# A gated product on one core: the first tile's first row is stored in two halves

## The chip, the cores and the metric

The kernel runs on one core of a Trainium2 chip. The metric is the device time of one execution in microseconds (us), the median of the runs shown. The core has engines that work side by side (VectorE, here DVE; ScalarE, ACT; GpSimd, POOL; SyncE, SP; TensorE is not used) and 16 DMA engines that move data between the chip's memory and the core's on-chip buffer. A transfer is issued by an engine's instruction stream, here SP's for loads and ACT's for stores, and signals on a semaphore when it has landed.

## The reference

```python
def reference(x):                       # x: 8192 x 8192, float32
    a, b = np.split(x, 2, axis=-1)
    return a * (1 / (1 + np.exp(-b)))   # 8192 x 4096, float32
```

Each row of `x` has 8192 numbers. The first half is multiplied by the sigmoid of the second half. 268.4 MB are read and 134.2 MB written.

## The kernel before, in words

**Tiles.** The 8192 rows are cut into 32 tiles of 256 rows (L20). A tile lies on the 128 partitions of the on-chip buffer, two rows of `x` to a partition (`R = 2`), so a tile's load is 8 MB (64 KB to a partition) and its store 4 MB (32 KB to a partition). There are two input slots `x_sb0`, `x_sb1` and two output slots `o_sb0`, `o_sb1`; tile i uses slot i mod 2 (`SLOTS = 2`).

**Pieces.** A tile's work, loads and stores are cut in units of which a tile has eight: 0 to 4 is the first row of every partition, 4 to 8 the second. For tiles 1 to 30 the load is one transfer, the work is two pieces (3/16 of the columns and the other 13/16, over both rows), and the store is one transfer. Tile 0 is loaded in two transfers of a row each, worked in four pieces of half a row each (`fourths`) and stored in two transfers of a row each. The last tile is worked in fourths too and stored in three transfers: a row, half a row, half a row.

**One piece** (`work`, L72): ACT replaces the second half of the row by its sigmoid, in place (L82), then DVE multiplies both halves into the output slot (L84). From tile 2 on POOL does the product of the smaller piece in place of DVE.

**What waits for what.** The order of instructions on each engine is the order in which the program writes them (`place` keeps program order), and `place` declares which waits are kept:

- A load of tile i + 2 (L63, issued by SP) waits for the products of tile i that read the same slot. The first three transfers, tile 0's two and tile 1's one, wait for nothing.
- A sigmoid waits for the load of its piece. For tiles 1 to 30 it also waits for the store of tile i - 2 that last read this output slot, if there is one; so tile 2's sigmoid waits for all of tile 0's stores, tile 3's for tile 1's store, and so on.
- A product waits for its sigmoid.
- A store (L68, issued by ACT's stream) waits for the products that it stores. ACT's stream is in order: while a store's issue waits for a product, the sigmoids behind it wait too.

**The order of the stores.** After piece k of a tile the loop at L98 issues those stores that are ready, but never after the last piece; the rest are issued after the next load. `behind[i]` (L36) says how many pieces a store's issue is held back: with 0 a store is issued as soon as the last piece that it needs has been written to the program, with 1 it is issued one piece later, so that the sigmoid of the following piece stands ahead of it in ACT's stream. For tile 0 (`behind` 0) the order on ACT is: sigmoid 0, sigmoid 1, store of row 0, sigmoid 2, sigmoid 3, store of row 1. For the last tile `behind` is 1.

`_launch_early` moves the very first load ahead of the program's entry barrier; `_close_on_sync` shortens the end of the program, in which SP waits for the last store. Neither is touched.

Of the kernel before, what the change touches and what calls it, by code (L numbers as in the profile page):

```python
# [8 lines left out]
def _tiles(ctx, tc, x, out):  # L9
    nc = tc.nc  # L10
    P = nc.NUM_PARTITIONS
    DEP = mybir.DependencyInfo(mybir.DependencyClass.Sync, mybir.DependencyReason.DATA)
    fp32 = mybir.dt.float32
    SIG = mybir.ActivationFunctionType.Sigmoid

    n_rows, n_cols = x.shape
    half = n_cols // 2
    R = 2
    SLOTS = 2
    n_tiles = n_rows // (P * R)  # L20
    x_t = x.rearrange("(n p r) m -> n p (r m)", p=P, r=R)
    out_t = out.rearrange("(n p r) m -> n p (r m)", p=P, r=R)

    pool = ctx.enter_context(tc.tile_pool(name="io", bufs=1))
    xs = [pool.tile([P, R * n_cols], fp32, name=f"x_sb{k}") for k in range(SLOTS)]
    os = [pool.tile([P, R * half], fp32, name=f"o_sb{k}") for k in range(SLOTS)]

    whole = [(0, 8)]
    rows = [(0, 4), (4, 8)]
    cut = half // 16 * 3  # L30
    few_and_most = [(0, 8, 0, cut), (0, 8, cut, half)]
    fourths = [(k, k + 2, k % 4 * half // 4, (k % 4 + 2) * half // 4) for k in range(0, 8, 2)]
    loads = [whole] * n_tiles
    works = [few_and_most] * n_tiles
    stores = [whole] * n_tiles
    behind = [0] * n_tiles  # L36
    loads[0] = stores[0] = rows
    works[0] = works[-1] = fourths
    stores[-1] = [(0, 4), (4, 6), (6, 8)]
    behind[-1] = 1  # L40

    def meet(a, b):
        return a[0] < b[1] and b[0] < a[1]

    traced = [[] for _ in range(SLOTS)]
    load_of, mul_of, store_of = {}, {}, {}

    def place(i, ins, *needs):


        kept = {n.ins.name for n in needs}
        for e in traced[i % SLOTS]:
            if e.ins.name not in kept:
                tc.declare_no_dep(ins.ins, e.ins, reason="follows from the waits that are kept")
        traced[i % SLOTS].append(ins)
        tc.keep_in_program_order(ins)
        return ins

    def load(i):
        for lo, hi in loads[i]:  # L60
            c = slice(lo * n_cols // 4, hi * n_cols // 4)
            free = [m for w, m in mul_of.get(i - SLOTS, []) if meet(w, (lo, hi))]
            ins = nc.sync.dma_start(out=xs[i % SLOTS][:, c], in_=x_t[i, :, c])  # L63
            load_of.setdefault(i, []).append(((lo, hi), place(i, ins, *free)))

    def store(i, lo, hi):
        c = slice(lo * half // 4, hi * half // 4)
        ins = nc.scalar.dma_start(out=out_t[i, :, c], in_=os[i % SLOTS][:, c])  # L68
        done = [m for w, m in mul_of[i] if meet(w, (lo, hi))]
        store_of.setdefault(i, []).append(((lo, hi), place(i, ins, *done)))  # L70

    def work(i, lo, hi, near, far):  # L72

        rows = xs[i % SLOTS].rearrange("p (r h m) -> p r h m", r=R, h=2)
        packed = os[i % SLOTS].rearrange("p (r m) -> p r m", r=R)
        r, c = slice(lo // 4, (hi + 3) // 4), slice(near, far)
        b = rows[:, r, 1, c]
        landed = [s for w, s in load_of[i] if meet(w, (lo, hi))]
        gone = [s for w, s in store_of.get(i - SLOTS, []) if meet(w, (lo, hi))]
        by_sigmoid = 0 < i < n_tiles - 1  # L80
        needs = [*landed, *(gone if by_sigmoid else ())]
        sig = place(i, nc.scalar.activation(out=b, in_=b, func=SIG), *needs)  # L82
        engine = nc.gpsimd if far == cut and i > 1 else nc.vector
        mul = engine.tensor_mul(out=packed[:, r, c], in0=rows[:, r, 0, c], in1=b)  # L84
        if by_sigmoid:
            for s in gone:
                tc.add_manual_dep(sig.ins, s.ins.name, DEP, reason="frees the output slot")
        place(i, mul, sig, *(() if by_sigmoid else gone))
        mul_of.setdefault(i, []).append(((lo, hi), mul))

    for i in range(SLOTS):
        load(i)
    for i in range(n_tiles):
        due = list(stores[i])
        for k, piece in enumerate(works[i]):
            work(i, *piece)
            ready = works[i][k - behind[i]][1] if k >= behind[i] else 0
            while len(stores[i]) > 1 and k < len(works[i]) - 1 and due[0][1] <= ready:  # L98
                store(i, *due.pop(0))
        if i + SLOTS < n_tiles:  # L100
            load(i + SLOTS)
        for lo, hi in due:
            store(i, lo, hi)
# [71 lines left out]
@with_exitstack  # L175
def kernel(
    ctx: ExitStack,
    tc: tile.TileContext,
    x: bass.AP,
    out: bass.AP,  # L180
):
    nc = tc.nc
    with ExitStack() as pools:
        _tiles(pools, tc, x, out)
    tc.close()
    tc.compile()
    _launch_early(nc)
    _close_on_sync(nc)
# [30 lines left out]
```

## Time and profile before

| | |
|---|---|
| median of 3 runs | 932.69 us (932.61 to 932.69) |
| span of the profiled execution, first to last instruction | 931.2 us |
| the profiled execution's own time | not given apart from its span; the median of the runs lies 1.5 us over it |
| DVE busy | 232.5 us (25%) |
| ACT busy | 229.8 us (25%) |
| POOL busy | 99.8 us (11%) |
| moved by DMA | 402.67 MB, 432 GB/s over the span |
| chain that ended last | DMA 75%, DVE 12%, ACT 12% |
| one tile of 32, in the middle | 29.0 us |

The start, as the timeline shows it: the sigmoids of tile 0's first row run from 12.05, its two products from 14.00 to 18.49, and its store is issued at 18.52. The second row's sigmoids run from 21.77, its products from 23.71 to 28.21, and at 28.23 both its store and the load of tile 2 are issued. Tile 1's sigmoid begins at 46.36, tile 2's at 70.87, tile 3's at 99.80.

How to read it: an engine's busy time is the sum of its instructions. The row named DMA shows in 40 slices how busy the 16 DMA engines were, in tenths. Queue q1 holds the loads, q10 the stores. "Us to landing" is the time from a transfer's issue until its semaphore says that all has landed. The chain is followed back from the last instruction, at each step to what released it; a link "DMA out_dram<-o_sb" lasts from the issue of a store to its landing. A packet is what one DMA engine moves at a time; in this kernel it is what one partition contributes to a transfer: 64 KB for a whole load, 32 KB for a row's load or a whole store, 16 KB for a row's store, 8 KB for half a row's.

### The profile page before, as it was taken

The numbers are of one execution on the slowest core, as the hardware profiler recorded it, in microseconds if no ns is written. First come the engines' busy times: TensorE is split into PE (matmuls) and PEld (weight loads), VectorE is DVE, ScalarE is ACT, GpSimd is POOL, SyncE is SP. The second block draws the span as 40 slices with busy tenths as digits, with TensorE's granted clock in tenths as the row PEclk, the third lists the DMA queues.
The fourth block names the chain that finished last, engine by engine and source line by source line (L and its number), as shares of the span: only waits on it lengthen the run. The fifth ranks groups of instructions, "written<-read, shape, count | busy, mean of one in ns | idle before, by whom it ended". The sixth has DMA issues, their size and how long they took to land.

```text
span 931.2 us, 325 instructions
## 1 busy us (share of the span) xinstructions
DVE 232.5 (25%) x39; ACT 229.8 (25%) x69; POOL 99.8 (11%) x33
## 2 busy tenths in 40 slices
DVE  1133311333113331133321333203332033320233
ACT  2123332033320333203332023320233302333023
POOL 0001111011110111101111011110111101111010
DMA  9999999999999999999999999999999999999998
GB/s 405 450 417 439 428 450 415 460 408 428 450 428 450 405 470 409 428 450 425 453 405 442 436 428 450 415 460 408 428 450 426 452 410 463 411 428 450 425 453 383
DMA packets 9793, 402.67 MB, mean 432 GB/s; under 512 B 1088, under 2 KB 1088, under 8 KB 1088
## 3 DMA queue, kind: packets, MB, share of 16 engines
q1 hardware_dynamic: 4752, 268.44, 66.6%
q10 hardware_dynamic: 5040, 134.22, 33.4%
q14 instruction: 1, 0.01, 0.0%
HBM read 268.44 MB, written 134.22 MB: 432 GB/s over the span
## 4 chain that ended last, share of the span: by engine, by line
DMA 75%; DVE 12%; ACT 12%; issue 0%; ACTq 0%; SPq 0%
DMA out_dram<-o_sb 65%; DVE o_sb L84 12%; ACT x_sb L82 12%; DMA x_sb<-in_x_dram 10%; ACTq L68 0%; SPq L63 0%
## 5 line engine op out<-in xcount | busy, mean ns | idle before, releaser
L84 DVE TENSOR_TENSOR o_sb<-x_sb 128x6656 f32<-128x6656 f32 (+2 forms) x39 | 232.5, 5970 | 690.3 <-ACT x_sb L82 690.3
L82 ACT ACTIVATE x_sb<-x_sb 128x1536 f32<-128x1536 f32 (+1 forms) x68 | 228.5, 3407 | 690.0 <-DMA out_dram<-o_sb 630.0
L84 POOL TENSOR_TENSOR o_sb<-x_sb 128x1536 f32<-128x1536 f32 x29 | 99.6, 3435 | 787.9 <-ACT x_sb L82 787.9
L82 ACT ACT_TABLE_LOAD x1 | 1.3, 1283 | 0.8 <-PEq L203 0.8
L203 POOL MEMSET const-float32-0.0<- 128x1 f32 x1 | 0.1, 98 | 0.2 <-issue 0.2
L203 POOL MEMSET const-bfloat16-1.0<- 128x1 bf16 x1 | 0.1, 101 | 0.0
L203 POOL MEMSET const-uint8-127<- 128x1 uint8 x1 | 0.1, 101 | 0.0
L203 POOL MEMSET const-float32-1.0<- 128x1 f32 x1 | 0.1, 98 | 0.0
## 6 DMA issues: line engine op xcount, KB each, us to landing
out_dram<-o_sb ACTq DMA_DIRECT2D x30, 4096.0 KB, 43.6
x_sb<-in_x_dram SPq DMA_DIRECT2D x2, 4096.0 KB, 16.5
out_dram<-o_sb ACTq DMA_DIRECT2D x3, 2048.0 KB, 28.0
out_dram<-o_sb ACTq DMA_DIRECT2D x2, 1024.0 KB, 8.3
x_sb<-in_x_dram SPq DMA_DIRECT2D x31, 43.5
```

The lines of the kernel that those rows point to most:

```text
L82: sig = place(i, nc.scalar.activation(out=b, in_=b, func=SIG), *needs)
L84: mul = engine.tensor_mul(out=packed[:, r, c], in0=rows[:, r, 0, c], in1=b)
L203: nc = _bacc.Bacc("TRN2", target_bir_lowering=False, num_devices=1)
```

## The change

Tile 0 is stored in three transfers instead of two: the first half of row 0 (units 0 to 2), the second half of row 0 (2 to 4), and row 1 (4 to 8). `behind[0]` becomes 1. The order on ACT becomes: sigmoid 0, sigmoid 1, store of the first half of row 0 (waits for product 0), sigmoid 2, store of the second half of row 0 (waits for product 1), sigmoid 3, store of row 1 (waits for products 2 and 3, and is issued after the load of tile 2 as before). Loads, works and all other tiles stay as they are. Tile 2's sigmoid now waits for three stores of tile 0 instead of two.

```diff
     behind = [0] * n_tiles
-    loads[0] = stores[0] = rows
+    loads[0] = rows
+    stores[0] = [(0, 2), (2, 4), (4, 8)]
     works[0] = works[-1] = fourths
     stores[-1] = [(0, 4), (4, 6), (6, 8)]
-    behind[-1] = 1
+    behind[0] = behind[-1] = 1
```

## The prediction

> **What bounds the kernel now.** I read the page first, then the stretches of the DMA, then the chain, then the landing of single transfers, and last the DMA in windows as narrow as one packet, because the change only moves transfers.
>
> ```profile
> DVE 232.5 (25%) x39; ACT 229.8 (25%) x69; POOL 99.8 (11%) x33
> DMA  9999999999999999999999999999999999999998
> DMA packets 9793, 402.67 MB, mean 432 GB/s; under 512 B 1088, under 2 KB 1088, under 8 KB 1088
> q1 hardware_dynamic: 4752, 268.44, 66.6%
> q10 hardware_dynamic: 5040, 134.22, 33.4%
> ```
>
> No engine is busy more than 25%; the DMA row has no hole. Loads (queue q1) and stores (q10) fill the 16 DMA engines to 66.6 + 33.4 = 100%. So an order of transfers alone can neither win nor lose time, unless it leaves the DMA engines with nothing to do. The two stretches after one another, each of two tiles, show the same rate:
>
> ```profile
> 114.14:172.15 58.01, 14.18 (x2) 14.25 (x4) 6.87 (x2) 1.00 1.00 434
> 172.15:230.15 58.00, 14.19 (x2) 14.24 (x4) 6.87 (x2) 1.00 1.00 434
> ```
>
> The last two numbers are DMA share and GB/s. The chain names another thing, ACT waiting for a store:
>
> ```profile
> 60.64 39.14 DMA out_dram<-o_sb
> 99.78 0.02 issue
> 99.80 7.13 ACT x_sb L82 x2
> 106.94 0.02 issue
> 106.96 7.10 DVE o_sb L84
> ```
>
> That is the loop that a late store would lengthen: a tile's sigmoid waits for the store that frees its output slot, and the tile's last product, 0.02 + 7.13 + 0.02 + 7.10 = 14.27 us later, releases the load of the tile after next (with the issue 14.33: landing 99.78, issue 114.11). In these 14.3 us the DMA engines live on what is queued. Next, how the two queues share. Each row here is a transfer with its median time to landing, taken from windows around 18.5, 28.2 and, for the last two, 918.2 and 920.4 us:
>
> ```profile
> out_dram<-o_sb ACTq DMA_DIRECT2D x1, 2048.0 KB, 28.0
> ...
> out_dram<-o_sb ACTq DMA_DIRECT2D x1, 2048.0 KB, 42.6
> x_sb<-in_x_dram SPq DMA_DIRECT2D x1, 42.4
> ...
> out_dram<-o_sb ACTq DMA_DIRECT2D x1, 2048.0 KB, 8.1
> ...
> out_dram<-o_sb ACTq DMA_DIRECT2D x1, 1024.0 KB, 8.3
> ```
>
> A store of 2 MB and a load of 8 MB, issued together at 28.23, land together (70.8 and 70.6). The queues do not share by bytes: they take turns, one packet each on each engine, and every transfer here is 8 packets per engine, whatever its size. The narrow windows from 23.6 to 24.2 and from 24.2 to 26.6 show the turns:
>
> ```profile
> q10 hardware_dynamic: 16, 0.26, 101.8%
> ...
> q1 hardware_dynamic: 16, 1.05, 101.2%
> ```
>
> Sixteen store packets of 16 KB, one per engine, then sixteen load packets of 64 KB. Hence the unit for all that follows: **a transfer costs 8 turns, and half the bytes cost just as many turns.**
>
> **Length of a turn.** First row load, landing 12.03, second 21.74: 9.71 us for 8 turns, 1.21 for 32 KB. A tile's period 29.0 us over 8 pairs is 3.63, so 2.42 for 64 KB beside 1.21. At the end (landings to a hundredth, as the trace holds them) the 2 MB store lands at 926.29, 4.85 us after the one before it (921.44): 0.61 for 16 KB. The last two, of 1 MB, land 2.45 and 2.43 us apart: 0.306 for 8 KB.
>
> **The change part by part.**
>
> *ACT's issues.* One issue more, 0.36 to 0.38 us of ACT's queue by its rows. The first store is now issued behind the first product: 14.00 + 2.25 (half of DVE's 4.49 for two) + 0.02 = 16.27 instead of 18.52. Behind it stands the third sigmoid, which waits for the second row load until 21.77: hidden. The second store stands between the third and fourth sigmoids (near 24) and waits for a product long done; the fourth sigmoid comes 0.38 us later, while DVE still works on the third product (2.25): hidden to within 0.1. SP's queue gets nothing new; the load of tile 2 is issued near 28.5, while q1 holds the load of tile 1 until past 43, so a delay there costs nothing.
>
> *Bytes.* The same. Sixteen more completion packets cost nothing seen (9793 packets for the whole, no hole in the row). Two transfers of 8 KB packets take 2 x 2.45 = 4.90 instead of 4.85: 0.05 us.
>
> *Turns.* Tile 0's stores need 24 turns instead of 16. That is the substance: the last store of tile 0 (call it C) lands a whole load later, and tile 2's sigmoid waits for C. Before, 16 turns began after the first packet of tile 1's load and ended with the end of tile 2's load, 70.79; all of tile 3's load was then still ahead as cover. Now C ends among tile 3's packets, and those left are the cover, with tile 1's store (8 x 1.21 = 9.68), already queued.
>
> *How many are left* hangs on the turn at which the first store gets in. The trace has one such entry. Store issued at 18.52; the load turns at 19.74 and 20.96 went by without it; it got in at 23.64 (first engine). So the entry takes more than 2.44 and at most 5.12 us. From 16.27 the turn at 18.54 (2.27 later) is just excluded; the turn at 19.74 is 3.47 later, the one at 20.96 is 4.69 later. The lower half of the bounds is likelier, as the first load of all had packets on the move about 1 us after its issue; I take 19.74, just ahead of the second row load's last packet. From there q1 has 1 + 8 + 8 + 8 = 25 packets to the end of tile 3's load. C's last is the 24th store turn, before the 24th load packet: 2 load packets are left.
>
> *The sum.* Cover left at C's end: 2 x 2.42 + 9.68 = 14.52 us. Against it: C's end to its landing 0.98 (tile 1's store: completion packets from 98.80, landing 99.78), landing to issue of tile 4's load 14.33, issue to full flow 1.60 (first load: issued at 0.0, its second packets, of 1.21, from 2.81). Together 16.91. The DMA engines idle 16.91 - 14.52 = **2.39 us**, once, near 98.5 to 100.9. In time: C lands near 19.74 + 9.74 (24 store turns) + 1.21 + 22 x 2.42 + 0.98 = 84.9 instead of 70.8, tile 4's load is issued near 99.2 instead of 85.2. From there load and store start together again, in step as before, and nothing is queued later that could give the time back: the row is full to the end. At the end, the last tile's first store is issued at 918.23 while tile 30's runs to 921.44, so that cover stays.
>
> The restart is bounded by 0.98 (first packets seen) and 1.98 (second packets of the last engine from 3.19), so idle 1.8 to 2.8. The profiled execution has a span of 931.2; the median of the three runs is 932.69, 1.5 more, lying around the span and untouched. Forecast 932.69 + 2.39 = 935.1.
>
> The Trainium skill (DMA: Bandwidth & Descriptors, Anatomy of one DMA) gives a transfer a fixed cost of about 2.0 us beside its bytes; one transfer more would then be 934.7, an estimate from that page. The last two stores here, 2.45 and 2.43 us apart for 8 turns, leave no room for it between queued transfers.
>
> **Rivals.**
>
> *One turn later (20.96).* Only 1 load packet is left as cover: idle 4.81, 937.5 (936.9 to 937.9). For it: 4.69 lies inside the bounds, and if one engine in sixteen enters late, C's landing is the late one. Still later (after the first packet of tile 1's load): 7.2, 939.9; it needs over 4.69 of at most 5.12.
>
> *Not slower: the store is caught a turn earlier, at 18.54.* Then 3 load packets are left, 16.94 against 16.91: no idle, 932.7. It decides at an entry of 2.27 us or less; the trace excludes up to 2.44, by 0.17 us, less than the 0.4 over which the engines' turns are spread. The same 932.7 holds if a turn is more than a packet per engine. The Trainium skill (same page, Queues, rings and completion order) lets a queue drain about 9 to 17 descriptors in its turn, which would pass a whole store at once and give 932.7; the 16 packets of 0.26 MB between two load turns speak against it here.
>
> *The fixed cost of a queued transfer.* Taken as the first load's 12.03 - 9.68 = 2.35: 935.0, but at the start and with no hole near 99. The rows of the end speak against it.
>
> *Faster.* Tile 1's load lands about 2 us earlier (46.3 to 44.2) because smaller packets stand between its own. If that reached the end: 930.6. Against it: full DMA row, so that what lands early pushes other bytes back.
>
> **How the numbers follow.** Forecast 0.52; one turn later 0.32; still later 0.04; not slower 0.09 (0.01 of it for the longer turn); fixed cost 0.01; faster 0.02. A measurement of this kernel can tell about 0.2%, 1.9 us, so slower means over 934.6: that takes an idle of 1.9, which fails only if the restart is near its lower bound (0.08 of the forecast's 0.52). Slower 0.44 + 0.32 + 0.04 + 0.01 = 0.81, same 0.08 + 0.09 = 0.17, faster 0.02. The range takes the first two cases with the restart's bounds: 934.4 (idle 1.8) to 938.0; it leaves out about 0.15.
>
> **What would show it.** Right: first store landing near 38.9 (19.74 + 2.45 + 1.21 + 6 x 2.42 + 0.98; 41.3 in the first rival), tile 1's load near 44, C landing near 85 (87.4 in the first rival), the load of tile 4 issued near 99.2 (101.6), a stretch near 98.5 to 101 with hardly any DMA, 29.0 us per tile on either side, and the end later by just that hole. Wrong: C landing before 83, or a full row through 100 us; or a loss elsewhere, as of 29.0 becoming more per tile, which would mean that the two queues stay out of step and that this costs something that I price at nothing.

## The result and the profile after

The changed kernel takes 938.74 us (median of 5 runs, 938.46 to 940.9) against 932.69 (5 runs, 932.49 to 932.71): 6.05 us more, a ratio of 1.0069 with a 95% interval of 1.0058 to 1.008. The ratios here and below compare the fast runs alone (a run over 1.5% above the fastest of its kernel is left out), so they can differ a little from the quotient of the medians, here 1.0065. Slower was forecast, and where the time goes was forecast; how much was not: 938.74 lies above the range, which ended at 938.0. The profiled execution of the changed kernel took 938.74, its span is 937.4.

The page after: the DMA row is full but for one slice, the fifth, and the store queue has 144 packets more (128 data packets of the third transfer and 16 that report completion).

```profile
DMA  9999899999999999999999999999999999999998
...
q10 hardware_dynamic: 5184, 134.22, 33.2%
```

The stretches of the changed kernel around that slice, then two tiles further on (the last two numbers are DMA share and GB/s; a packet is counted whole where it starts, so a share can pass 1):

```profile
97.00:99.00 2.00, 2.00 (x1) 0.00 (x0) 0.00 (x0) 1.00 1.02 442
99.00:101.00 2.00, 2.00 (x1) 0.00 (x0) 0.00 (x0) 1.00 0.00 0
101.00:103.00 2.00, 1.40 (x1) 0.06 (x1) 0.00 (x0) 1.00 0.00 0
103.00:105.00 2.00, 0.00 (x0) 2.00 (x2) 0.50 (x1) 1.00 1.95 524
105.00:107.00 2.00, 0.00 (x0) 2.00 (x1) 2.00 (x1) 1.00 0.00 0
...
134.00:192.00 58.00, 14.18 (x2) 14.24 (x4) 6.88 (x2) 1.00 1.00 434
```

From 99 to 103 no data packet starts. Then one packet per engine starts, and these packets take 1.95 x 2, or 3.9 us each, where a 64 KB packet in flow takes 2.42. From 134 on two tiles take 58.0 us as before. So the loss is one hole.

The chain of the changed kernel has, in the place of the store of tile 1, a wait of which the profile does not name the transfer; it ends at 87.99, which is the landing of tile 0's last store:

```profile
58.87 0.36 ACTq L69
59.23 28.75 another core or an unknown queue
...
88.15 7.13 ACT x_sb L83 x2
```

Tile 2's sigmoid begins at 88.15; before it began at 70.87. The transfers issued in the windows around 16.3, 22.8 and 29.3 us, with their time to landing:

```profile
out_dram<-o_sb ACTq DMA_DIRECT2D x1, 1024.0 KB, 25.3
...
out_dram<-o_sb ACTq DMA_DIRECT2D x1, 1024.0 KB, 40.6
...
out_dram<-o_sb ACTq DMA_DIRECT2D x1, 2048.0 KB, 58.7
x_sb<-in_x_dram SPq DMA_DIRECT2D x1, 38.2
```

The second half row, 1 MB, is 40.6 us on its way, and tile 0's second row, issued together with a load four times its size, lands 20.5 us after it. Before, those two landed together.

**Which turn it was.** The windows 20.1 to 20.62 and 84.3 to 84.7 of the changed kernel:

```profile
q1 hardware_dynamic: 5, 0.16, 79.8%
q10 hardware_dynamic: 11, 0.09, 40.9%
...
q10 hardware_dynamic: 5, 0.08, 47.7%
```

When the first store got in, 11 engines moved a store packet ahead of the second row load's last packet and 5 engines moved that packet first. The same number of engines, 5, have their last packet of tile 0's stores one turn later than the others, at 84.3 to 84.7 (the other 11 have theirs at 81.8 to 82.2). A transfer has landed when its last engine is done: the 5 decide.

**The hole, term by term.** In the trace the last store packets end at 99.33 (first engine). Landing 87.99 to issue of tile 4's load 102.46: 14.47. Issue to the first packets 103.43: 0.97; these take 1.49 longer than in flow. So 14.47 + 0.97 + 1.49 = 16.93 us stood against a cover of 99.33 - 87.99 = 11.34, and 5.59 us are lost. The spans differ by 6.2. Of the other 0.6 us, about 0.5 lies in stretched packets: those that start between 18.4 and 19.0 take 1.66 instead of 1.21, those between 62.7 and 63.7 about 2.7 instead of 2.42, against one such stretch (2.67, at 20.96) before: 0.45 + 0.30 - 0.25.

### The profile page after: what moved, and what is told of

Same layout as the page of the kernel before. It is cut to its first block, busy times and chain, and to the rows that moved or that the text cites. A ratio compares the mean times of both kernels' runs of the same rounds, so it can differ in the third digit from the quotient of the medians.

```text
span 937.4 us, 328 instructions
## 1 busy us (share of the span) xinstructions
DVE 232.5 (25%) x39; ACT 229.8 (25%) x69; POOL 100.0 (11%) x33
## 4 chain that ended last, share of the span: by engine, by line
DMA 70%; DVE 13%; ACT 13%; another core or an unknown queue 3%; issue 0%; ACTq 0%; SPq 0%
DMA out_dram<-o_sb 61%; DVE o_sb L85 13%; ACT x_sb L83 13%; DMA x_sb<-in_x_dram 9%; ACTq L69 0%; SPq L64 0%; ACTq L83 0%
## 6 DMA issues: line engine op xcount, KB each, us to landing
out_dram<-o_sb ACTq DMA_DIRECT2D x30, 4096.0 KB, 43.6
x_sb<-in_x_dram SPq DMA_DIRECT2D x31, 43.5
```

## The experiments

The theory is that of turns: tile 0 now needs 24 store turns, its last store lands so late that too few load packets are left as cover, and the time lost is about 8.0 - 2.42 x (load packets of tile 3 left), where 8.0 is the measured 16.93 plus 0.76 between the end of the load packet ahead of the store's completion packets (87.23, first engine) and the landing, less the 9.68 of tile 1's store. With one packet left this is 5.6, the measured hole. The rivals: the early issue itself costs; or a third transfer, or its small packets, has a price of its own.

**Two stores, the first still early.**

```diff
-    stores[0] = [(0, 2), (2, 4), (4, 8)]
+    stores[0] = [(0, 2), (2, 8)]
```

> Tile 0 in two stores, the first of them the half row that the change issues early, the second the other three quarters. Theory of turns: 16 store turns instead of 24, so the last store of tile 0 lands before the load of tile 2, tile 3's load still stands ahead as cover, no hole near 100 us: 932.7 to 933.3. Rival, the early half row itself costs (it takes turns from the second row load and shifts the start): the loss of 6 us stays, near 938.7. Rival, any sort of new packet size or order on ACT costs: also near 938.7.

Measured 934.15 (ratio 1.0017, 1.0007 to 1.0026). The hole near 100 is gone, with the half row still issued at 16.39: neither the early issue nor the packet size makes it. But 1.5 us are left, more than expected. The stretches of this kernel show where:

```profile
99.00:101.00 2.00, 0.00 (x0) 0.00 (x0) 0.00 (x0) 1.00 0.91 393
...
921.00:922.00 1.00, 1.00 (x2) 0.36 (x1) 0.00 (x0) 1.00 0.01 0
```

Full near 100, and a hole of its own at 921 to 922. In this kernel the stores run ahead of the loads: all through the middle a store takes 38.8 us to land and the load issued with it 43.6, where before it was 43.6 and 43.5. So when the last load lands (914.76), most of tile 30's store is done, and the last tile's first store, issued at 921.25, comes 0.85 us before tile 30's lands (922.10). Before it came 3.2 us ahead (918.23 against 921.44).

**Three stores, nothing early.**

```diff
-    stores[0] = [(0, 2), (2, 4), (4, 8)]
+    stores[0] = [(0, 4), (4, 6), (6, 8)]
```

> Tile 0 in three stores, but a row first and then two half rows; nothing is issued earlier than before (the first store about 3 us later, behind the third sigmoid's start at 21.8). Theory of turns: 24 store turns that begin near 25.8, when 6 + 8 + 8 load packets are left; all of tile 3's load is over when the last store of tile 0 lands, cover is tile 1's store alone, the hole is 2.42 us longer than in the changed kernel (5.6 measured there, so 8.0): 940.7 to 941.4. Rival, the early issue is what costs: no loss, 932.7.

Measured 941.22 (1.0092, 1.0077 to 1.0107). The first store is issued at 21.68, later than in the kernel before, and the loss is larger, as the count of turns has it. Tile 0's last store lands at 90.49, 0.3 us after tile 3's load. The stretches of this kernel:

```profile
99.00:101.00 2.00, 2.00 (x1) 0.00 (x0) 0.00 (x0) 1.00 0.00 0
...
103.00:105.00 2.00, 1.90 (x1) 0.00 (x0) 0.00 (x0) 1.00 0.00 0
105.00:107.00 2.00, 0.00 (x0) 1.56 (x2) 0.00 (x0) 1.00 1.84 524
```

The first packets after the hole start at 105.92 instead of 103.43: 2.5 us later than in the changed kernel, about one load packet (2.42).

**Three stores, and one more load.**

```diff
-    loads[0] = rows
+    loads[0] = loads[1] = rows
```

> The changed kernel with all three stores of tile 0, and tile 1 loaded in two transfers of a row each: 8 turns more for the load queue too. Theory of turns: after the entry 33 load packets stand against 24 store turns, the last store of tile 0 lands with the load of tile 2, 8 to 9 load packets are left as cover, no hole: 932.7 to 933.3, though a transfer is added and none removed. Rival, every transfer more costs something of its own: over 938.7. Rival, the early half row costs: 938.7.

Measured 933.88 (1.0011, 1.0001 to 1.002), 0.6 us above what was expected and 4.9 us less than the changed kernel, with a transfer more. Eight turns added on the load side give back what eight turns added on the store side took. The store of tile 0's second row now lands before the load issued with it:

```profile
out_dram<-o_sb ACTq DMA_DIRECT2D x1, 2048.0 KB, 39.2
x_sb<-in_x_dram SPq DMA_DIRECT2D x1, 44.0
```

What is left above 932.7, 1.2 us, is mostly the hole at the end again: its stretch from 921 to 922 has a DMA share of 0.01 too, and closing it (the last experiment) brings 0.7 us.

**One more store in the middle.** The edit is to the kernel before:

```diff
     behind[-1] = 1
+    stores[15], behind[15] = rows, 1
```

> The kernel before, with tile 15 alone stored in two transfers of a row each, both issued where the one was. Nothing at the start is touched. Theory of turns: its second store lands at the end of tile 18's load instead of tile 17's, tile 17's sigmoid waits for it, and tile 16's store (9.7 us) is the only cover: one hole of 8.0 us, between the landing and tile 19's load, 29.0 us per tile on either side: 940.5 to 941.2. Rival, the start is what is sensitive: 932.7. Rival, a transfer more costs about 2 us: 934.7.

Measured 941.16 (1.0091, 1.0076 to 1.0106). The start is untouched, and a hole of the same kind opens some 435 us later. The stretches of this kernel:

```profile
475.00:533.00 58.00, 7.56 (x2) 14.24 (x4) 6.88 (x2) 1.00 1.00 434
532.00:534.00 2.00, 1.47 (x1) 0.50 (x1) 0.00 (x0) 1.00 0.61 262
534.00:536.00 2.00, 2.00 (x1) 0.00 (x0) 0.00 (x0) 1.00 0.00 0
...
538.00:540.00 2.00, 1.63 (x1) 0.00 (x0) 0.00 (x0) 1.00 0.00 0
...
580.00:638.00 58.00, 14.24 (x3) 14.25 (x4) 6.87 (x2) 1.00 1.00 434
```

Idle from 534.4 to 540.7, full on both sides. This settles that the loss is not one of the start: dividing one store in the middle costs as much as three late stores at the start. Other tiles were not tried.

**The first store later.**

```diff
-    behind[0] = behind[-1] = 1
+    behind[0], behind[-1] = 2, 1
```

> The changed kernel's three stores with behind 2 for tile 0: the first half row is issued behind the third sigmoid's start (near 21.8) instead of at 16.3, the other two after the load of tile 2. Theory of turns: the store enters near 25.8 instead of 20.1 to 21.4, when 22 load packets are left against 24 store turns; no load packet is left as cover, the hole grows from 5.6 to 8.0: 940.9 to 941.5, as the row and two half rows gave. Rival, issuing early is what costs: less than the changed kernel, towards 932.7.

Measured 941.01 (1.0089, 1.0074 to 1.0104). With the same three stores, issuing the first one later (at 21.69; the second at 22.14, ahead of the load of tile 2 and not behind it as expected) makes it worse, not better. The early issue is the helpful half of the change.

**Four stores.**

```diff
-    stores[0] = [(0, 2), (2, 4), (4, 8)]
+    stores[0] = [(0, 2), (2, 4), (4, 6), (6, 8)]
```

> Tile 0 in four stores of half a row: 32 store turns. Theory of turns: once tile 3's load has ended nothing stands between the last stores, which then run back to back; the cover is tile 1's store alone, as with any count that outlasts tile 3's load: the hole saturates at 8.0: 940.9 to 941.5. Rival, each transfer over two costs the same: 932.7 + 2 x 6.05 = 944.8.

Measured 941.23 (1.0091, 1.0076 to 1.0106). No price per transfer: four stores cost what three late ones cost (941.22 and 941.01). Against the changed kernel the fourth store adds 2.5 us, but as a longer hole: the first packets after it start at 105.78 instead of 103.43. The Trainium skill (DMA: Bandwidth & Descriptors, Anatomy of one DMA) gives each transfer about 2.0 us beside its bytes, a figure for transfers that GpSimd issues, where SP and ACT issue them here; between queued transfers these runs do not show it, since the fourth store adds 0.0 to 0.2 us to the three late ones.

**The first store earlier.** The first product is made of the raw halves:

```diff
-        sig = place(i, nc.scalar.activation(out=b, in_=b, func=SIG), *needs)
+        skip = i == 0 and lo == 0
+        sig = landed[0] if skip else place(i, nc.scalar.activation(out=b, in_=b, func=SIG), *needs)
```

> The changed kernel without the sigmoid of tile 0's first piece (the first product is of the raw halves, so this part of the result is left out): the first store is issued near 14.3, 2.0 us earlier, all transfers as in the changed kernel. Theory of turns: it enters before the second row load's seventh packet, near 18.4, on all engines; 3 load packets are left as cover when tile 0's last store lands, the hole shrinks from 5.6 to 5.6 - 2 x 2.42 = 0.8: 933.4 to 934.4; if one engine enters a turn later, 3.2: near 936.3. Rival, a fixed price for the third store or its small packets: 938.7 still.

Measured 937.85, 942.83, 952.7 and 965.41 in four runs (1.0082, 1.0051 to 1.0113, from the first two): not what was expected. But at the place in question the trace has what was expected: the store issued at 14.32, tile 0's last store landing at 82.99, tile 4's load issued at 97.46 and its first packets at 99.14, with no idle ahead of them. The time went elsewhere, so the kernel was run again.

> The kernel without the first piece's sigmoid once more (that part of the result is left out). In its first trace the hole near 99 was 0.9 us, as the theory of turns had it, but its tiles took 29.2 to 29.5 us instead of 29.0, and one of the 16 DMA engines ended 6 us behind the others. If that is a disturbance of that run, the time is now 933.4 to 934.4. If it comes with this kernel, because the load of tile 4 arrives just as the last store packets run out and the engines lose step, it is again over 937 and the start is again as before.

Measured 934.17 (1.0023, 1.0008 to 1.0038), as the first case had it. Two of its ten runs took 940.7 and 967.9. The stretches of this run:

```profile
97.00:99.00 2.00, 0.55 (x1) 0.00 (x0) 0.00 (x0) 1.00 0.95 410
99.00:101.00 2.00, 0.00 (x0) 0.72 (x1) 0.00 (x0) 1.00 1.62 524
```

The 4 us without a transfer are gone; what is left is the slow first packet. Two microseconds in the issue of one store are worth 4.6 us of the whole, two load packets of cover, as the turns have it.

**The first store earlier, nothing left out.**

```diff
     works[0] = works[-1] = fourths
+    works[0] = [(0, 1, 0, half // 4), (1, 2, half // 4, half // 2), *fourths[1:]]
...
-    stores[0] = [(0, 2), (2, 4), (4, 8)]
+    stores[0] = [(0, 1), (1, 4), (4, 8)]
```

> Nothing left out: tile 0 in three stores, the first a quarter of a row, worked as a piece of its own, so that it is issued near 14.3 instead of 16.3; then three quarters of the row, then the second row. 24 store turns as in the changed kernel. Theory of turns: the first store enters near 18.4 to 18.9, 2 to 3 load packets are left as cover at the landing of tile 0's last store, hole 0.8 to 3.2 instead of 5.6: 933.4 to 936.3. Rival, a fixed price for a third store: 938.7.

Measured 938.4, 942.43, 946.0 and 965.2 in four runs (1.0102, 1.0066 to 1.0139, from the first three): not what was expected either. Again the start does as expected (store issued at 14.47, tile 0's last store landing at 83.16, tile 4's load issued at 97.64, its stretches near 100 like those above), and again the time goes later. The end of this kernel:

```profile
922.00:924.00 2.00, 1.68 (x1) 2.00 (x2) 0.00 (x0) 1.00 0.23 98
924.00:926.00 2.00, 2.00 (x2) 1.89 (x2) 0.00 (x0) 1.00 0.08 33
926.00:928.00 2.00, 2.00 (x2) 0.76 (x1) 0.00 (x0) 1.00 0.36 156
```

A share of 0.06 is one engine of 16. Fifteen engines have nothing to do from about 922 to 928 while one still moves packets, and the last tile's first store is issued at 926.85. One engine has fallen behind the others, and since a transfer lands with its slowest engine, everything that waits is late: tile 31's load is issued and lands late against the work of the other fifteen. The lag begins where the loads start again: tile 1's store still lands within 0.4 us over the 16 engines (99.67 to 100.10), tile 4's load over 3.2 us (129.13 to 132.29), and transfers near 885 over 8 to 11 us. Why one engine loses step is not settled. Both kernels that show it in a trace issue tile 4's load just as the engines run out of packets; but the first of them, run again, issued it at the same place (97.61) and mostly did not show it, and the kernel before took 947.07 and 947.27 in two of its 65 runs beside these experiments, which have no trace. So that this moment is the cause is not shown.

**One store for tile 0.** The edit is to the kernel before:

```diff
-    loads[0] = stores[0] = rows
+    loads[0] = rows
```

> The kernel before with tile 0 in one store, issued after the load of tile 2 near 28.2: 8 store turns instead of 16, nothing issued early. Theory of turns: no hole near 99; the stores run ahead of the loads by some turns to the end, so that at the last load's landing less store work is left as cover and a hole of about 0.9 us opens near 921, as with the two-store kernel that began early: 933.2 to 934.3. Rival, fewer transfers are never worse: 932.7 or less.

Measured 935.33 (1.0028, 1.0017 to 1.0039). Fewer transfers, and 2.6 us slower than before; the expected place, but a larger hole, which goes on into the stretch from 922 to 924 (DMA share 0.31). One stretch at its end:

```profile
921.00:922.00 1.00, 1.00 (x1) 0.70 (x1) 0.00 (x0) 1.00 0.01 0
```

In the middle its stores take 34.8 us to land beside loads of 43.6: they run 8.8 us ahead, where the two-store kernel ran 4.8 ahead, and the last tile's first store is issued at 922.65, 0.5 us after tile 30's has landed. The size was missed because the lead was taken to be that of the two-store kernel.

**The end, mended.** Two stores of which the first is early, and the last tile's store cut so that its first part can go one product earlier:

```diff
-    stores[-1] = [(0, 4), (4, 6), (6, 8)]
+    stores[-1] = [(0, 2), (2, 4), (4, 6), (6, 8)]
```

> Tile 0 in two stores (half a row early, then three quarters), which gave 934.15, and the last tile stored in four half rows, so that its first store is issued one product (2.2 us) earlier, near 919. Theory: what that kernel lost beside the one before is mostly a hole of 0.9 to 1.5 us at 921.3 to 922.2: its stores run ahead of the loads, so the last load lands when less store work is left as cover. With the earlier store the hole closes: 932.6 to 933.3. Rival, the loss lies at the start or in the early half row: 934.1 still.

Measured 933.43 (1.0009, 0.9999 to 1.0019): 0.7 us less than without that edit, a tenth above what was expected. The same edit beside the three stores and tile 1's two loads:

> The changed kernel's three stores, tile 1 loaded in two rows (933.9 so far), and the last tile stored in four half rows, the first issued one product earlier. Theory: the first edit closed the hole near 99 us, and what was left was mostly a hole of 0.95 us at 921.1 to 922.1, where the stores, now ahead of the loads, leave less cover; the second edit closes that: 932.8 to 933.4. A third of a microsecond may stay from the stretched packets at the first store's entry. Rival, the early half row has a price of its own: 933.9 still.

Measured 933.19 (1.0007, 0.9998 to 1.0016), as expected. The hole at 921 is closed in both (DMA share of that stretch 0.88 and 0.95). The 0.5 to 0.8 us that stay above the kernel before are not accounted for. So the change itself can stay almost without loss, if the load queue gets as many turns as the store queue and the end has its cover. Nothing tried is faster than the kernel before: the DMA engines were full there, and the best these kernels reach is to fill them again.

## Why the prediction was wrong in size and right in kind

- **What bounds the kernel: right.** The tiles keep 29.0 us and 434 GB/s on either side of every hole, and time is lost only where the DMA engines have nothing to do.
- **A transfer costs 8 turns whatever its bytes: right for its data,** and shown by eight more turns of stores costing up to 8.6 us in both places tried, eight more turns of loads giving most of it back, and a fourth store costing nothing beside three late ones. The rule of a queue draining 9 to 17 descriptors in its turn (the Trainium skill, DMA: Bandwidth & Descriptors, Queues, rings and completion order) would have given 932.7; here it took one packet per engine each turn.
- **The packet that reports completion takes a turn too: not counted.** On the 5 late engines tile 0's last store packets end at 84.94 to 85.27, then a load packet goes, and only then come the completion packets of 4 bytes, at 87.35 to 87.69. So the landing came 2.7 us after the last packet's end, where the prediction had 0.98. The loads' completion packets take turns as well. The second row load's come at 21.7 to 22.4, and the window from 21.4 to 22.5 holds two store packets for each engine, with only that completion packet between them:

```profile
q10 hardware_dynamic: 32, 0.26, 56.2%
```

Up to the landing of tile 0's last store three completions of stores stand against three of loads. They cancel, so the forecast's times of landing could be near without this count; that much was luck.

- **The turn of entry: the step that failed first.** The forecast put the first store ahead of the second row load's last packet on all engines. It was so on 11 of 16; on the other 5 the store entered a turn later, and they set the landing: 87.99 instead of 84.9, 2.42 us of it for one load packet less of cover. That is the first rival, at 0.32, with "if one engine in sixteen enters late, C's landing is the late one" as its argument. Its landmarks are near those measured: first store landing at 41.5 (41.3), last store at 88.0 (87.4), tile 4's load issued at 102.5 (101.6).
- **The restart: the term that was mis-sized.** Priced at 1.60, at most 1.98, from the kernel's first load, whose first packets are 32 KB. Measured 2.46: 0.97 to the first packets, and these, of 64 KB, take 3.91 instead of 2.42. That is 0.86 more than the forecast and 0.48 above its bound; the first packets of 32 KB had cost only 0.61 over flow (1.82 for 1.21).
- **Priced at nothing:** 0.14 us in the issue (14.47 for 14.33) and about 0.5 us in stretched packets, 0.75 in two places less 0.25 in the one that the trace before had shown (2.67 for 2.42) and that was not counted.
- **The sum.** The rival's idle 4.81, 0.86 for the restart and 0.14 for the issue, less 0.22 (0.76 instead of 0.98 ahead of the landing), make 5.59, as measured. The rest, 0.5 us, is the stretches. With the right turn and the old restart the range would still have ended at 938.0, below 938.7.
- **The rivals.** Not slower (caught at 18.54) and faster did not come: tile 1's load did land earlier, 44.6 instead of 46.3, and this went no further. The fixed cost of a transfer fell with the four stores, and with tile 1's second load, a transfer more that saved 4.9 us.
- **The end:** "that cover stays" held for the changed kernel (924.37 against 927.59), but not for those in which the stores run ahead of the loads.

## What to carry to other kernels

Where two DMA queues are kept full, as here, count packets per engine, not bytes: in these traces they take turns packet by packet, so dividing a transfer on one queue held that queue back by up to a whole transfer of the other, and what waited for it was late by as much. Then ask what is still queued when the late waiter releases the next transfer; if it is less than the way from landing to new flow (here 16.9 us), the difference is lost once, and dividing a transfer on the other queue gave most of it back. A queue that runs ahead of its partner was no gain here either: it took its cover away from the end.

## What the runs showed that was not expected

A restart of idle DMA engines with 64 KB loads cost 1.49 us on the first packet beside the 0.97 us from issue to start; in three other kernels with such a hole the first packet cost 1.3 to 1.5 us. The Trainium skill (DMA: Bandwidth & Descriptors, Latency and other measured facts) has about 0.6 us to the first byte for such queues; the 0.97 here is a first packet's start as the trace records it, and the slow first packet is not in that figure.

A store issued beside a busy load queue got its first packet about 3.9 to 4.3 us later (16.29 to 20.14 to 20.6 on the engines that took it first), and the load packets just ahead of it were stretched (1.66 for 1.21 us). Engines differed enough to fall on both sides of a turn, so a time may move by 2.4 us from run to run, though no trace shows it: one run of the changed kernel took 940.9, the others 938.46 to 938.87, which would be one load packet less of cover; that run has no trace.

In two traces, of 942.83 and 942.43 us where 933.4 to 936.3 was expected, one DMA engine of 16 fell behind near 100 us and fell further behind to the end. The longer runs of these kernels have no trace. What starts it stays open.
